# Conditioning loads between the output weight tiles of the first FFN: one load per place, the gate's rows apart from its chunks, intervals of 0.88 tiles

## The chip, the cores and the metric

The kernel runs on one core of a Trainium2 chip. The time is device microseconds of one launch. The kernel before takes 1496.64 us, the median of three runs (1495.39 to 1496.93). One more execution was taken with the hardware profiler; all rows and times below come from it.

## What is computed

Two transformer blocks over 512 tokens of width 1024, in float32. Each block has a mixer (a gated linear recurrence in the first, dilated attention in the second) and a SwiGLU feed-forward layer (FFN). Six vectors per block, made from the conditioning input `c`, scale, shift and gate what goes in and out of the two halves:

```
cond = jax.nn.silu(c)
for layer in range(DEPTH):
    mod = (cond @ ada_w[layer] + ada_b[layer])[:, None, :]
    sh1, sc1, g1, sh2, sc2, g2 = jnp.split(mod, 6, axis=-1)
    u = rms_norm(h, norm_g[layer, 0]) * (1.0 + sc1) + sh1
    ...
    h = h + (1.0 + g1) * rms_norm(y, norm_g[layer, 1])
    u = rms_norm(h, norm_g[layer, 2]) * (1.0 + sc2) + sh2
    y = (jax.nn.silu(gate) * up) @ w_out          # gate, up = split(u @ w_in)
    h = h + (1.0 + g2) * rms_norm(y, norm_g[layer, 3])
```

A vector is a pair (layer, v), with v = 0 to 5 for sh1, sc1, g1, sh2, sc2, g2. The change concerns three of them, which are made while the first FFN (layer 0) multiplies by its output weights `ffn_w_out[0]`: the gate (0, 5), needed at the end of that FFN, and the scale (1, 1) and the shift (1, 0), needed when the attention's input is formed right behind it.

## The kernel before

**Products.** Matmuls run in a split form: a float32 operand x is cut into hi = round(x) (line 90, on ACT) and lo = x - hi (line 91, on DVE), and `three` (lines 586 to 588) adds hi x hi, lo x hi and hi x lo. The second half of the first FFN multiplies the 22 blocks of the hidden activations (`mid`, cut into `oh` by ACT at line 582 and `ol` by DVE at line 583, a ring of five) by 11 tiles of output weights, 1 MB each; the text calls them T0 to T10. A tile is 48 matmuls of 512 columns.

**The stream of weights.** `Stream` walks a fixed list of items. A weight item ("w") is loaded by SP into one of two raw buffers, cut by ACT and DVE into one of three pairs of parts, and then used by PE. Items that load nothing ("do") take no buffer. So with two raw buffers, an item's load is issued when the last reader of the item two loads earlier is done, and SP issues in the order of the list. ACT, DVE and POOL also work in a fixed order, which a scheduler sets when the program is built; from line 978 on, and at the ends of the FFNs, it is written out by hand (`manual_schedule`).

**Conditioning.** A vector's product with `ada_w` is cut into two halves of 512 columns and each half into two chunks of 512 rows, 1 MB each. A chunk takes a raw buffer and four DVE operations: one multiplies its first 128 rows by `cond` (line 401, or 403 if it continues a sum), the others multiply and add (line 403). After a half's second chunk POOL sums over the 128 partitions (line 405). Then comes a finishing step: for the gate, two rows (bias and norm weight, 512 columns each, broadcast to all partitions: two loads at line 64 into one raw buffer) and two DVE operations (lines 450 and 451); for the scale and the shift, four pairs of small DVE operations that turn the row into columns (line 415) and one or two that add the bias and the norm weight (lines 419 and 421).

The text calls the gate's chunks g00, g01 (first half), g10, g11 (second half) and its rows G0, G1; the second half of the scale's chunks s10, s11, with finishing step S1 (its first half is made earlier, between the FFN's input weights); the shift's chunks b00, b01, b10, b11 with finishing steps B0 and B1. V0 and V1 are the first two weight tiles of the attention, which follow in the list.

`weave(ws, others, first, every)` makes the list: after the weight tile with number i it puts the next groups of `others` for as long as i is at least `first` plus `every` times the number of groups already put:

```
for i, w in enumerate(ws):
    res.append(w)
    while i >= first + n * every and o:
        res += o.pop(0)
        n += 1
return res + [i for g in o for i in g]
```

For this place the list was

```
T0 g00 | T1 g01 | T2 g10 | T3 G0 g11 | T4 s10 | T5 G1 s11 | T6 b00 | T7 S1 b01 | T8 b10 | T9 B0 b11 | T10 B1 | V0 V1
```

**The turn.** At the end of the FFN (from `mm(0)` on) the order is written out. PE finishes token block t (`mm(t)`, which uses T9 and T10); ACT squares the result (line 622), DVE multiplies it by the gate (`yg`, line 631), POOL raises the sum to the power -1/2 (`rr`, line 637), DVE adds into the residual (`h`, line 647), ACT squares that, DVE and POOL make the next factor, DVE scales the block (`xn`, line 661), and PE transposes it (`flip(t)`, line 667, eight transposes). ACT and DVE then apply the scale and shift columns (lines 677 and 679), cut the result into `uh` and `ul` (lines 682 and 686), and PE multiplies it by V0 and V1 (`v_prod(t)`). The columns of (1, 0) and (1, 1) have to be complete before line 677 first runs. PE's order there is: mm(0), mm(1), first half of mm(2), flip(0), first half of mm(3), second half of mm(2), flip(1), second half of mm(3), v_prod(0), flip(2), v_prod(1), flip(3), v_prod(2), v_prod(3).

Of the kernel before, what the change touches and what calls it, by code (L numbers as in the profile page):

```python
# [301 lines left out]
def block_kernel(tc, x, c, positions, ada_w, ada_b, norm_g, hgrn_w_in, lower, hgrn_norm_g, hgrn_w_out,  # L302
# [8 lines left out]
    with ExitStack() as ctx:  # L311
# [150 lines left out]
        def ada_seq(*vecs):  # L462

            res, last = [], None
            for l, v in vecs:
                for hf in range(2):
                    res.append([ada_item(l, v, hf, 0)])
                    res.append(([fin_item(*last)] if last else []) + [ada_item(l, v, hf, 1)])
                    last = (l, v, hf)
            return res + [[], [fin_item(*last)]]  # L470

        def ada_halves(l, v):

            return [[ada_item(l, v, hf, kq)] for hf in range(2) for kq in range(2)], [fin_item(l, v, hf) for hf in range(2)]
# [11 lines left out]
        def weave(ws, others, first, every=1):  # L486

            res, o, n = [], list(others), 0
# [7 lines that stand above are left out]
        items = []  # L496
# [11 lines left out]
        def ffn_ws(l):  # L508

            a, w = [], ffn_w_in[l]  # L510
            for j in range(PLAIN[l]):
                a += [win(w, j * 256), win(w, DFF + j * 256)]
            for f in range(2 * PLAIN[l], NF):
                a.append(("quarters", tuple(w[:, c:c + P].rearrange("(k p) n -> p k n", p=P) for c in (DFF + f * P, f * P))))
            return a, [wrow(ffn_w_out[l], j) for j in range(NF // 2)]

        items += weave(hg, ada_seq((0, 2), (0, 4), (0, 3), (1, 4)), 1, 0.7) + hg_o
        f0a, f0b = ffn_ws(0)
        n0 = 2 * PLAIN[0]
        gate, gate_fins = ada_halves(0, 5)  # L520
        one, two = ada_seq((1, 1)), ada_seq((1, 0))
        items += weave(f0a[:n0], [one[0], one[1], [], one[3][:1]], 2) + f0a[n0:]
        late = [gate[0], gate[1], gate[2], gate_fins[:1] + gate[3], one[2], gate_fins[1:] + one[3][1:], two[0], one[5] + two[1]]
        items += weave(f0b, late + two[2:], 0, 0.95)
        AW = attn_w_in[0]

        def av(g, hf):
# [30 lines left out]
        late = ada_seq((1, 2), (1, 3))  # L558
# [780 lines left out]
        early, late = slice(0, 256), slice(256, S)  # L1339
# [1062 lines left out]
        for kind, g, i in order:  # L2402
            if kind == "v":
                steps += [("v", None, None, k, *p) for k, p in enumerate(value_unit(g - 1, i))]
            else:
                two = sevens(g, i) if by_seven(g) else plain(g, i)
# [120 lines left out]
```

## Time and profile before

| | |
|---|---|
| median of three runs | 1496.64 us |
| the profiled execution, its own time | 1492.7 us |
| its span, first to last instruction | 1491.0 us |
| PE busy | 1467.8 us |
| the output weights' part of the first FFN, T0 to mm(3) | 536.9 to 662.2 us of the span |
| PE's waits between 520 and 780 us | 3.8 us: 3.1 for lo of line 91, 0.7 for xn of line 661 |

A row of the timeline has the start, the time in us, the engine, the line of the code and the operation, what it writes and reads, how many are merged, and in brackets how long the engine had been idle before it and what released it. Engines: PE multiplies, ACT is ScalarE, DVE is VectorE, POOL is GpSimd, SPq is the queue from which loads are issued. A matmul of 512 columns is shown with 0.39 us but the next starts 0.227 us after it, since they overlap. T4 to T10 are the rows of line 90 at 576.33, 587.02, 598.99, 609.42, 618.59, 627.85 and 637.11 us, V0 that at 640.74 us.

### The profile page before, as it was taken

Reading aid. Unit: us, or ns where it says so; the run is one execution under the profiler, and the core shown is the slowest. Engines: PE = TensorE matmul, PEld = TensorE weight load, DVE = VectorE, ACT = ScalarE, POOL = GpSimd, SP = SyncE. Lnnn points to the kernel's source line nnn. Section 1 sums busy time; section 2 is a strip of 40 time slices with the busy share of each in tenths; the row PEclk is TensorE's granted clock in tenths of the full one; section 3 lists DMA queues with packets and bytes.
Section 4 is the critical chain, followed back from the end, with each engine's and each line's share of the span. In section 5 each row is a group of like instructions: output and inputs, shape, how many; then the busy total and the mean of one; then the engine's idle time right before and its main releaser. Section 6 shows DMA issues by size and latency. Waiting matters only on the chain. (4 is left out here: it accounts for less than half of the span.)

```text
span 1491.0 us, 25093 instructions
## 1 busy us (share of the span) xinstructions
PE 1467.8 (98%) x9835; PEld 1315.0 (88%) x9835; DVE 1090.9 (73%) x1796; ACT 793.6 (53%) x1470; POOL 191.2 (13%) x172
## 2 busy tenths in 40 slices
PE   8999999999999999999999999999999999999998
PEld 6777788888999988788998999999988899999886
DVE  4587678488688875777798877888776978887533
ACT  4433343373455542257647878567885555555231
POOL 1011112031111100131001010001012211110100
PEclk9999999999999999999999999999999999999999
DMA  9654554115334346644344443354352333334531
GB/s 308 183 175 132 193 170 165 62 59 167 86 114 114 114 149 206 218 141 142 111 118 123 135 121 93 86 163 126 88 199 82 112 88 114 114 114 144 193 116 57
DMA packets 210727, 201.08 MB, mean 135 GB/s; under 512 B 8824, under 2 KB 168496, under 8 KB 210352
## 3 DMA queue, kind: packets, MB, share of 16 engines
q1 hardware_dynamic: 207632, 192.71, 41.5%
q10 hardware_dynamic: 1952, 6.65, 1.2%
q8 instruction: 77, 1.26, 0.3%
q0 software_dynamic: 1024, 0.12, 0.2%
q14 instruction: 42, 0.34, 0.1%
HBM read 192.30 MB, written 5.30 MB: 133 GB/s over the span
## 5 line engine op out<-in xcount | busy, mean ns | idle before, releaser
L90 ACT CAST hi<-raw 128x2048 fp32r<-128x2048 f32 x43 | 82.3, 1913 | 149.3 <-DMA raw<-in_ffn_w_out_dram 78.0
L91 DVE TENSOR_TENSOR lo<-raw,hi 128x2048 fp32r<-128x2048 f32 x43 | 101.8, 2370 | 65.6 <-ACT hi L90 65.6
L586 PE MATMUL ps_mm<-uh,hi 128*128 128x512 f32 (+1 forms) x400 | 145.4, 364 | 0.0
L587 PE MATMUL ps_mm<-ul,hi 128*128 128x512 f32 (+1 forms) x400 | 144.3, 361 | 1.1 <-DVE ul L686 1.1
L588 PE MATMUL ps_mm<-uh,lo 128*128 128x512 f32 (+1 forms) x400 | 143.7, 359 | 0.0
L1988 PE MATMUL ps_mm<-apart,hiq 128*128 128x256 f32 (+1 forms) x608 | 142.3, 327 | 0.3 <-ACT xs L2103 0.2
L1988 PEld LDWEIGHTS ps_mm<-apart,hiq 128*128 128x128 f32 x608 | 99.9, 189 | 8.8 <-ACT xs L2103 0.7
L1988 PE MATMUL ps_mm<-apart,loq 128*128 128x256 f32 (+1 forms) x304 | 97.5, 321 | 0.5 <-DVE loq L2125 0.5
L958 DVE TENSOR_TENSOR loq<-raw,hiq 128x1024 fp32r<-128x1024 f32 x68 | 80.2, 1221 | 22.3 <-ACT hiq L954 22.3
L967 PE MATMUL ps_mm<-th,hiq 128*128 128x256 f32 x340 | 93.8, 276 | 0.0
L967 PE MATMUL ps_mm<-tl,hiq 128*128 128x256 f32 x340 | 93.8, 276 | 0.0
L967 PE MATMUL ps_mm<-th,loq 128*128 128x256 f32 x340 | 93.8, 276 | 0.0
L586 PEld LDWEIGHTS ps_mm<-uh,hi 128*128 128x128 f32 x400 | 75.1, 188 | 18.3 <-issue 6.7
L587 PEld LDWEIGHTS ps_mm<-ul,hi 128*128 128x128 f32 x400 | 75.3, 188 | 12.3 <-DVE ul L686 1.5
L588 PEld LDWEIGHTS ps_mm<-uh,lo 128*128 128x128 f32 x400 | 75.1, 188 | 12.4 <-issue 1.1
L587 PE MATMUL ps_mm<-lo,oh 128*128 128x512 f32 x208 | 81.2, 390 | 3.1 <-DVE lo L91 3.1
L938 POOL TENSOR_TENSOR raw<-raw 128x512 f32<-128x512 f32 x34 | 44.9, 1320 | 301.8 <-DVE loq L934 142.5
L586 PE MATMUL ps_mm<-hi,oh 128*128 128x512 f32 x208 | 81.1, 391 | 0.0
L954 ACT CAST hiq<-raw 128x1024 fp32r<-128x1024 f32 x68 | 68.1, 1047 | 20.8 <-DVE raw L942 19.2
L1988 PE MATMUL ps_mm<-uh,hiq 128*128 128x256 f32 x256 | 71.8, 281 | 0.0
L1988 PE MATMUL ps_mm<-ul,hiq 128*128 128x256 f32 x256 | 71.2, 278 | 0.0
L1988 PE MATMUL ps_mm<-uh,loq 128*128 128x256 f32 x256 | 71.2, 278 | 0.0
(484 smaller groups left out, 4612.9 us busy)
## 6 DMA issues: line engine op xcount, KB each, us to landing
raw<-in_ada_w_dram SPq DMA_DIRECT2D x40, 1024.0 KB, 5.1
raw<-in_ffn_w_in_dram SPq DMA_DIRECT2D x136, 256.0 KB, 4.1
raw<-in_ffn_w_out_dram SPq DMA_DIRECT2D x22, 1024.0 KB, 4.9
raw<-in_attn_w_in_dram SPq DMA_DIRECT2D x64, 256.0 KB, 4.6
raw<-in_hgrn_w_in_dram SPq DMA_DIRECT2D x12, 1024.0 KB, 5.3
raw<-in_attn_w_in_dram SPq DMA_DIRECT2D x12, 1024.0 KB, 5.2
raw<-in_ffn_w_in_dram SPq DMA_DIRECT2D x10, 1024.0 KB, 6.3
raw<-in_attn_w_in_dram SPq DMA_DIRECT2D x16, 512.0 KB, 4.6
```

Source lines behind the costliest of these rows:

```text
L90: self.nc.scalar.copy(hi, t)
L91: self.nc.vector.tensor_sub(lo, t, hi.bitcast(F32))
L586: pe.matmul(ps, ah, bh, start=start, stop=False, skip_group_check=part)
L587: pe.matmul(ps, ah, bl, start=False, stop=False, skip_group_check=part)
L588: pe.matmul(ps, al, bh, start=False, stop=stop, skip_group_check=part)
L938: pool.tensor_add(r[:, 2], r[:, 2], r[:, 0])
L954: act.copy(hi, src)
L958: dve.tensor_sub(lo, src, hi.bitcast(F32))
L967: pe.matmul(ps, w[x][:, a], us[kt][y], start=begin and kt + m == 0, stop=kt == 3 and m == 2, skip_group_check=True)
L1988: pe.matmul(dst(), x, y, start=begin and i == 0, stop=i == len(todo) - 1, skip_group_check=True)
```

## The change

The gate's rows G0 and G1 become groups of their own instead of being put with the chunk behind them, and the spacing goes from 0.95 to 0.88 tiles, since there are now two groups more:

```diff
-        late = [gate[0], gate[1], gate[2], gate_fins[:1] + gate[3], one[2], gate_fins[1:] + one[3][1:], two[0], one[5] + two[1]]
-        items += weave(f0b, late + two[2:], 0, 0.95)
+        late = [gate[0], gate[1], gate[2], gate_fins[:1], gate[3], one[2], gate_fins[1:], one[3][1:], two[0], one[5] + two[1]]
+        items += weave(f0b, late + two[2:], 0, 0.88)
```

The list becomes

```
T0 g00 | T1 g01 | T2 g10 | T3 G0 | T4 g11 | T5 s10 | T6 G1 | T7 s11 | T8 b00 S1 b01 | T9 b10 | T10 B0 b11 B1 | V0 V1
```

No instruction is added or taken away. What moves is the order of the loads on SP, and with it the order of ACT's, DVE's and PE's work on them. Three places follow, before and after; a name such as `raw_5302` is a buffer of one build, and its number differs between the two.

The first place is SP's queue from G0 to T6. Before (G0 in two loads, g11, T4, s10, T5, G1 in two loads, s11, T6):

```order
L64 DMA raw_5202<-in_ada_b_dram 128x512
L64 DMA raw_5202<-in_norm_g_dram 128x512
L70 DMA raw_5209<-in_ada_w_dram 128x4x512
L70 DMA raw_5302<-in_ffn_w_out_dram 128x2x1024
L70 DMA raw_5309<-in_ada_w_dram 128x4x512
L70 DMA raw_5315<-in_ffn_w_out_dram 128x2x1024
L64 DMA raw_5377<-in_ada_b_dram 128x512
L64 DMA raw_5377<-in_norm_g_dram 128x512
L70 DMA raw_5384<-in_ada_w_dram 128x4x512
L70 DMA raw_5444<-in_ffn_w_out_dram 128x2x1024
```

Now (G0 in two loads, T4, g11, T5, s10, T6, G1 in two loads):

```order
L64 DMA raw_5202<-in_ada_b_dram 128x512
L64 DMA raw_5202<-in_norm_g_dram 128x512
L70 DMA raw_5209<-in_ffn_w_out_dram 128x2x1024
L70 DMA raw_5302<-in_ada_w_dram 128x4x512
L70 DMA raw_5308<-in_ffn_w_out_dram 128x2x1024
L70 DMA raw_5371<-in_ada_w_dram 128x4x512
L70 DMA raw_5377<-in_ffn_w_out_dram 128x2x1024
L64 DMA raw_5439<-in_ada_b_dram 128x512
L64 DMA raw_5439<-in_norm_g_dram 128x512
```

T4 stands one load earlier, T5 one, and T6 two (a chunk and G1).

The second place is SP's queue from T8 to V0. Before (T8, b10, T9, b11, T10, V0):

```order
L70 DMA raw_5525<-in_ffn_w_out_dram 128x2x1024
L70 DMA raw_5598<-in_ada_w_dram 128x4x512
L70 DMA raw_5604<-in_ffn_w_out_dram 128x2x1024
L70 DMA raw_5666<-in_ada_w_dram 128x4x512
L70 DMA raw_5672<-in_ffn_w_out_dram 128x2x1024
L70 DMA raw_5744<-in_attn_w_in_dram 128x4x512
```

Now (T8, b00, b01, T9, b10, T10, b11, V0):

```order
L70 DMA raw_5512<-in_ffn_w_out_dram 128x2x1024
L70 DMA raw_5575<-in_ada_w_dram 128x4x512
L70 DMA raw_5581<-in_ada_w_dram 128x4x512
L70 DMA raw_5643<-in_ffn_w_out_dram 128x2x1024
L70 DMA raw_5660<-in_ada_w_dram 128x4x512
L70 DMA raw_5666<-in_ffn_w_out_dram 128x2x1024
L70 DMA raw_5728<-in_ada_w_dram 128x4x512
L70 DMA raw_5734<-in_attn_w_in_dram 128x4x512
```

Two chunks stand between T8 and T9, b11 stands behind T10 instead of ahead of it, and as many loads as before stand ahead of V0.

The third place is DVE's queue where the turn begins. Before, B1 (the four pairs of line 415 and line 419) stands ahead of V0's lo (line 91), and then comes the first gating (line 631):

```order
L415 ISA diag_5808,cols<-shared,ident 128x128
L415 ISA cols 128x1
L415 ISA diag_5810,cols<-shared,ident 128x128
L415 ISA cols 128x1
L415 ISA diag_5812,cols<-shared,ident 128x128
L415 ISA cols 128x1
L415 ISA diag_5814,cols<-shared,ident 128x128
L415 ISA cols 128x1
L419 TENSOR_TENSOR cols<-cols,adab 128x4
L91 TENSOR_TENSOR lo_5818<-raw_5744,hi_5817 128x2048
L631 TENSOR_TENSOR yg_5866<-ps_mm_5095,gate_5299 128x512
```

Now b11's four operations (line 403) and V0's lo come first, and B1 is spread through the turn's first block:

```order
L403 SCALAR_TENSOR_TENSOR shared<-raw_5728,cond,shared 128x512 x4
L91 TENSOR_TENSOR lo_5818<-raw_5734,hi_5817 128x2048
L415 ISA diag_5808,cols<-shared,ident 128x128
L415 ISA cols 128x1
L415 ISA diag_5810,cols<-shared,ident 128x128
L415 ISA cols 128x1
L631 TENSOR_TENSOR yg_5866<-ps_mm_5095,gate_5299 128x512
L415 ISA diag_5812,cols<-shared,ident 128x128
L415 ISA cols 128x1
L635 TENSOR_SCALAR rv_5868<-ss_5861 128x1
L631 TENSOR_TENSOR yg_5872<-ps_a_5099,gate_5299 128x512
L415 ISA diag_5814,cols<-shared,ident 128x128
```

Two pairs of B1 moved behind V0's lo and ahead of the first gating, one pair to between the gating and the factor, and the last, with line 419, behind the second gating.

## The prediction

> **What bounds the kernel now.** I read the page's totals first, then the windows around the change, then PE's timeline where it stands still, and last the queues that feed it.
>
> ```profile
> PE 1467.8 (98%) x9835; PEld 1315.0 (88%) x9835; DVE 1090.9 (73%) x1796; ACT 793.6 (53%) x1470; POOL 191.2 (13%) x172
> ...
> 536.90:640.00 103.10, 101.12 (x447) 83.27 (x445) 71.55 (x109) 31.02 (x33) 16.19 (x5) 1.00 0.61 206
> 640.00:652.00 12.00, 10.89 (x49) 8.79 (x48) 10.22 (x22) 5.83 (x13) 1.44 (x3) 1.00 0.56 178
> 652.00:676.00 24.00, 23.25 (x120) 19.33 (x118) 17.79 (x38) 17.34 (x44) 11.24 (x17) 1.00 0.14 45
> ```
>
> PE is busy 98% of the span, so the kernel is a string of matmuls and an edit that removes none can win back only PE's idle time. In the output weights' stretch (first window: length, then PE's busy time) that is 2 us of 103; in the first 12 us of the turn 1.1 us. Where it lies:
>
> ```profile
> 604.59 0.50 PE L587 MATMUL ps_mm<-lo,oh 128*128 128x512 f32 x1 [1.98 <-DVE lo L91]
> 641.39 0.50 PE L587 MATMUL ps_mm<-lo,oh 128*128 128x512 f32 x1 [1.11 <-DVE lo L91]
> 652.19 0.60 PE L667 MATMUL ps_mm<-ident,xn 128*128 128x128 f32 x4
> 667.60 0.60 PE L667 MATMUL ps_mm<-ident,xn 128*128 128x128 f32 x4
> 674.84 0.66 PE L667 MATMUL ps_mm<-ident,xn 128*128 128x128 f32 x4 [0.75 <-DVE xn L661]
> ```
>
> PE waits 1.98 us for T6's lo and 1.11 us for T10's, 3.1 us together: all that the change can win. The last three rows are flip(0), flip(2) and flip(3). What do the flips have to spare? DVE's rows of the turn:
>
> ```profile
> 641.86 0.29 DVE L415 CUSTOM_DVE_ANT_0 diag<-shared,ident 128x128 f32<-128x128 f32 x1
> ...
> 643.20 0.16 DVE L419 TENSOR_TENSOR cols<-cols,adab 128x4 f32<-128x4 f32 x1
> 643.27 2.29 DVE L91 TENSOR_TENSOR lo<-raw,hi 128x2048 fp32r<-128x2048 f32 x1
> 645.48 0.68 DVE L631 TENSOR_TENSOR yg<-ps_mm,gate 128x512 f32<-128x512 f32 x1
> 646.21 0.68 DVE L631 TENSOR_TENSOR yg<-ps_a,gate 128x512 f32<-128x512 f32 x1
> 647.01 1.42 DVE L647 SCALAR_TENSOR_TENSOR h<-yg,rr,h 128x512 f32<-128x512 f32 x2
> 650.16 0.75 DVE L661 TENSOR_SCALAR xn<-h,rr 128x1024 f32<-128x1024 f32 x1 [0.67 <-POOL rr L637]
> 666.58 0.75 DVE L661 TENSOR_SCALAR xn<-h,rr 128x1024 f32<-128x1024 f32 x1
> ```
>
> xn(0) ends at 650.91 and PE comes to flip(0) at 652.19: 1.3 us to spare. xn(2) ends at 667.33, flip(2) is at 667.60: 0.3 us. For xn(3) PE waits 0.75 us. So by the end of the turn **the bound is the chain of DVE, ACT and POOL through the turn**, not PE, and that chain starts where V0's lo ends (643.27 + 2.29) and the first gating begins. A PE that reaches the turn earlier finds the same chain. What counts is when the chain starts and how long its first steps are.
>
> **The load stream.** SP's issues (g11's, then T5's with G1 behind it, then T7 to V0, b00 among them), and ACT's cuts of T5, T8 and V0:
>
> ```profile
> 567.54 0.38 SPq L70 DMA_DIRECT2D raw<-in_ada_w_dram  x1
> ...
> 580.82 0.37 SPq L70 DMA_DIRECT2D raw<-in_ffn_w_out_dram  x1
> 584.30 0.34 SPq L64 DMA_DIRECT2D raw<-in_ada_b_dram  x1
> ...
> 604.57 0.37 SPq L70 DMA_DIRECT2D raw<-in_ffn_w_out_dram  x1
> 608.40 0.37 SPq L70 DMA_DIRECT2D raw<-in_ada_w_dram  x1
> 613.69 0.37 SPq L70 DMA_DIRECT2D raw<-in_ffn_w_out_dram  x1
> ...
> 622.86 0.37 SPq L70 DMA_DIRECT2D raw<-in_ffn_w_out_dram  x1
> ...
> 632.11 0.37 SPq L70 DMA_DIRECT2D raw<-in_ffn_w_out_dram  x1
> 635.61 0.37 SPq L70 DMA_DIRECT2D raw<-in_attn_w_in_dram  x1
> ...
> 587.02 1.92 ACT L90 CAST hi<-raw 128x2048 fp32r<-128x2048 f32 x1 [5.96 <-DMA raw<-in_ffn_w_out_dram]
> 618.59 1.91 ACT L90 CAST hi<-raw 128x2048 fp32r<-128x2048 f32 x1 [6.22 <-DMA raw<-in_ffn_w_out_dram]
> 640.74 1.91 ACT L90 CAST hi<-raw 128x2048 fp32r<-128x2048 f32 x1 [1.20 <-DMA raw<-in_attn_w_in_dram]
> ```
>
> T8 is issued at 613.69 and its cast starts at 618.59: 4.9 us. Cast 1.9 and lo 2.3 us later its buffer is free, and T9 is issued at 622.86: 9.2 us a tile, as from T9 to T10 (9.25). So the stream runs at the round trip of a tile's buffer, the chunk in the other buffer being hidden in it, as long as one load stands between two tiles.
>
> **Part 1, one load per place.** G1 and a chunk between T3 and T6 go behind them. T4 takes the place that g11 had (567.54); at 9.2 us each T5 follows at 576.7, T6 at 585.9, T7 at 595.1 (before: 604.57), T8 at 604.3. Every lo is then ready before PE asks; T6's and T10's waits go: **PE gains 3.1 us up to the turn**, and comes to flip(0) at 652.19 - 3.1 = 649.1.
>
> **Part 2, two chunks behind T8.** With 0.88, b00 and b01 fall into one place. b01 goes into T8's buffer when its lo is done (604.3 + 9.2 = 613.5). T9 must wait for b00's four operations, which stand behind T8's lo, one cut of `mid` (0.6 us) and mixed with S1:
>
> ```profile
> 605.06 0.28 DVE L415 CUSTOM_DVE_ANT_0 diag<-shared,ident 128x128 f32<-128x128 f32 x1
> ...
> 608.30 0.15 DVE L419 TENSOR_TENSOR cols<-cols,adab 128x4 f32<-128x4 f32 x1
> ```
>
> The same mixture took 3.3 us here, so T9 is issued at about 613.5 + 0.6 + 3.3 = 617.5, T10 at 626.7, and V0, in the same buffer, at 636. Before it was 635.61: **the 9 us that the stream had won at T7 are gone at V0**, since as many loads lie ahead of it. V0 then lands 5.1 us later (as 635.61 to 640.74) at 641.1, its cast ends at 643.0, and its lo starts there or, with eight round trips at up to 9.25 us, 0.4 to 0.6 us later; before it started at 643.27. Term: +0.2 us. The other end: if T9 were issued right behind b01, V0 would come 3.5 us sooner, but B1 stands ahead of the first gating and has to wait for POOL's sum (643.1, part 3); the first gating could then start at 643.9 instead of 645.48, and less the other 0.4 us of B1 the chain would win 1.1 us. I take +0.2, the buffers' own time.
>
> **Part 3, B1 moves into the chain.** Four pairs at 0.33 us (a quarter of 641.86 to 643.20) and line 419: 1.4 us. Before they ran ahead of V0's lo, where DVE would have had to wait for V0's cast till 642.65 in any case. Now two pairs (0.66) stand ahead of the first gating, one (0.33) ahead of the factor, and the last behind the second gating, where DVE waits 0.2 us for POOL anyway (646.21 + 0.60 to 647.01), so 0.1 of it counts. Term: **+1.1 us**. Its sum over partitions must be ready:
>
> ```profile
> 633.26 2.32 DVE L403 SCALAR_TENSOR_TENSOR shared<-raw,cond,shared 128x512 f32<-128x512 f32 x3
> 635.67 3.24 POOL L405 PARTITION_ALL_REDUCE shared<-shared  x1 [14.58 <-DVE shared L403]
> ```
>
> T10's lo ends at 635.9, one cut (0.6) and b11's four operations (0.77 each) follow to about 639.8, POOL takes 3.2 us to 643.1, and the first pair is due at 645.6. If that cover of 2.5 us were gone, each us late would be a us of the chain.
>
> **Part 4, what the new neighbours cost.** G1 is now issued 3 us behind T6. Before it stood 3.5 us behind T5, which took 6.2 us to land (580.82 to 587.02) instead of 4.9. Bounds 0 and 1.3 us, nothing below; I take 0.6. And POOL's sums:
>
> ```profile
> 576.40 3.23 POOL L405 PARTITION_ALL_REDUCE shared<-shared  x1 [19.13 <-DVE shared L403]
> 600.15 3.23 POOL L405 PARTITION_ALL_REDUCE shared<-shared  x1 [20.51 <-DVE shared L403]
> ...
> 578.27 2.52 DVE L91 TENSOR_TENSOR lo<-raw,hi 128x2048 fp32r<-128x2048 f32 x1 [2.05 <-ACT hi L90]
> 600.94 3.59 DVE L91 TENSOR_TENSOR lo<-raw,hi 128x2048 fp32r<-128x2048 f32 x1 [0.89 <-ACT hi L90]
> ```
>
> A lo beside a sum took 2.52 us (1.4 us together) and 3.59 us (2.4 us together) instead of 2.29. In the new order S1's sum (from 608.5) and B0's (from 622) reach 0.6 us each into the lo of T8 and T9. Bounds 0 and 1.3 us; at this overlap nearer the first row: 0.3 us for both. The Trainium skill ("SBUF — State Buffer", "Who interferes with whom") says that a DVE operation with two SBUF inputs and a GpSimd one that reads SBUF share a port pair and that the loser blocks fully. By that the 3.59 would have been 4.7, so the trace does not agree in size; by the rule this term would be 1.2 and the sum 0.9 higher.
>
> **The sum.** 0.2 + 1.1 + 0.6 + 0.3 = 2.2 us later through the chain, which carries flip(2) and flip(3); the 3.1 us that PE wins turn into a wait of 653.1 - 649.1 = 4.0 us at flip(0). Behind flip(3) the queues are in the old order and PE is full, so the 2.2 us stay. The profiled execution would go from 1492.7 to 1494.9; the median stands 3.9 us above that execution, and I add the same 2.2 us: **1498.8 us**.
>
> **The rivals.**
>
> *PE keeps what it wins* (1493.5 us; part of it, 1495.5). For it: both waits do go. Against: flip(2) and flip(3) wait for xn already, and V0 has as many loads ahead. Whole gain 0.05, the early V0 of part 2 (gain up to 1.1) or a zero 0.10.
>
> *The clock falls in the new wait* (slower, decided at flip(0)).
>
> ```profile
> 1484.09 0.39 PE L588 MATMUL ps_b<-hi,ol 128*128 128x512 f32 x1
> ...
> 1486.00:1488.40 2.40, 0.00 (x0) 0.00 (x0) 1.52 (x3) 0.00 (x0) 0.13 (x1) 0.99 0.26 97
> 1488.40:1491.00 2.60, 0.00 (x0) 0.00 (x0) 0.00 (x0) 0.00 (x0) 0.00 (x0) 0.50 0.30 112
> ```
>
> The last matmul ends at 1484.48, and the granted clock is 0.99 until 1488.4 and 0.50 after it: it halved 3.9 us after PE stopped. The new wait is 4.0 us, at the point from which this decides. No row shows a return; if the half rate lasts as long as the fall took, 3.9 us, it costs 1.9 us, of which PE has about 1.0 to spare before flip(2) (653.1 + 15.4 = 668.5 against xn(2) at 669.5). So 2.2 + 0.9 = 3.1, 1499.7 us, and 1501 if it stays twice as long. Chance 0.22. The Trainium skill ("TensorE: Matmul & The Clock Gate", Part 1) has the clock gated to half after an idle window of 3.4 us that runs freely, and released after one busy window; the trace's 3.9 us agree, and by it the cost would be 1.7 us before the spare time.
>
> *The stretch of lo and loads is at its upper bounds* (1.3 for G1, 1.3 for a lo): 0.2 + 1.1 + 2.6 = 3.9, 1500.5 us. For it: each was seen once at that size. Chance 0.15.
>
> *The edit doesn't do what it says*: it holds for T0 to T7, not for T8; that is in the forecast.
>
> **How the numbers follow.** Forecast 0.48, of which 0.08 lies over +3 us. 0.2% (3 us) is about what a measurement of this kernel can tell from no change. Slower by more: 0.08 + 0.19 of the clock + 0.15 = 0.42. Faster by more: 0.05. Within: 0.53. The likeliest case alone spans 1497.4 to 1500.2; with the early V0 below and clock and stretch above the range is 1495.6 to 1501.6.
>
> **What would show it.** No wait for lo of line 91 in T4 to T10; T8's issue near 604 and T9's 13 us behind it; V0's lo starting at 643 to 645; line 415 between the two gatings; a wait of 3.5 to 5 us for xn at flip(0) and about 1 us at flip(2) and flip(3). I am wrong if V0's lo starts before 642, if flip(0) waits under 2 us, or if flip(3) comes earlier than 674.8.

## The result, and the profile after

The changed kernel takes 1500.87 us (median of 7 runs, 1498.13 to 1502.85) and the kernel before 1496.64 us (7 runs beside it, 1495.27 to 1498.14): ratio 1.0032, 95% interval 1.0022 to 1.0041. A second measurement on another chip gave 1.0033 (1.0020 to 1.0045). The change makes the kernel 4 to 5 us slower. The time lies in the forecast range (1495.6 to 1501.6), but 2.1 us above the forecast of 1498.8: not the case called likeliest (within 0.2% of before) came, but the one with 0.42 (slower by more).

The profiled execution took 1500.58 us (span 1498.9). T3's lo, the last tile before the lists differ, ran at 565.22 before and runs at 567.94 now, so this execution was 2.7 us behind before the change had done anything: the granted clock was halved twice for 3.4 us, at 15 and 152 us, which the profiled execution of before does not show. All comparisons below are therefore counted from T3's lo.

PE's waits between 520 and 700 us (the view of waits: who waited for what, us, times, longest):

```profile
engine line waited for: us in total, times, longest us
PE ps_mm L667 <- DVE xn L661: 7.0, 1, 7.0
```

Both waits for lo of line 91 are gone, as forecast, and in their place stands one of 7 us for xn(0), where 4.0 was forecast. PE's rows of flip(0) to flip(3), first four transposes of each:

```profile
657.85 1.11 PE L667 MATMUL ps_mm<-ident,xn 128*128 128x128 f32 x4 [6.97 <-DVE xn L661]
...
667.12 0.60 PE L667 MATMUL ps_mm<-ident,xn 128*128 128x128 f32 x4
...
676.17 0.60 PE L667 MATMUL ps_mm<-ident,xn 128*128 128x128 f32 x4
...
682.52 0.60 PE L667 MATMUL ps_mm<-ident,xn 128*128 128x128 f32 x4
```

From T3's lo, flip(0) came at 86.97 us before and comes at 89.91 now, flip(2) at 102.38 and 108.23, flip(3) at 109.62 and 114.58: 2.9, 5.9 and 5.0 us later. The transposes of flip(0) last 1.11 us instead of 0.60. The windows around them (length, then busy time of PE, PEld, DVE, ACT and POOL, then the granted clock, the DMA share and GB/s) say why:

```profile
640.00:650.88 10.88, 10.88 (x49) 8.66 (x47) 7.10 (x14) 3.07 (x5) 3.23 (x1) 1.00 0.67 202
650.88:653.61 2.73, 0.00 (x0) 0.00 (x0) 0.38 (x3) 0.00 (x0) 0.34 (x1) 1.00 0.94 354
653.61:657.85 4.24, 0.00 (x0) 0.00 (x0) 2.51 (x6) 2.54 (x8) 0.81 (x2) 0.50 0.00 0
657.85:663.85 6.00, 6.00 (x18) 5.06 (x19) 4.83 (x11) 3.79 (x10) 1.42 (x3) 0.50 0.00 0
```

The clock falls to half 2.7 us after PE stopped and stays there for 10.24 us, 6.0 of them with PE at work. That was a rival of the prediction. Of the 3.0 us by which the wait is longer than the 4.0 forecast, 0.9 come from a PE that is earlier than forecast; the other 2.0 are a chain that is 4.2 us late instead of 2.2, and the largest part of that was not in the prediction. POOL's last sum and the first factor (`rr`) of the turn:

```profile
643.13 3.23 POOL L405 PARTITION_ALL_REDUCE shared<-shared  x1 [14.37 <-DVE shared L403]
653.27 0.59 POOL L637 TENSOR_TENSOR rr<-rv,expo 128x1 f32<-128x1 f32 x1 [6.91 <-issue]
```

and DVE's rows of the same place, from V0's lo to xn(0), and xn(2):

```profile
646.68 2.29 DVE L91 TENSOR_TENSOR lo<-raw,hi 128x2048 fp32r<-128x2048 f32 x1 [3.64 <-ACT hi L90]
...
649.44 0.68 DVE L631 TENSOR_TENSOR yg<-ps_mm,gate 128x512 f32<-128x512 f32 x1
...
650.25 0.21 DVE L635 TENSOR_SCALAR rv<-ss 128x1 f32<-128x1 f32 x1
650.37 0.68 DVE L631 TENSOR_TENSOR yg<-ps_a,gate 128x512 f32<-128x512 f32 x1
...
653.90 1.41 DVE L647 SCALAR_TENSOR_TENSOR h<-yg,rr,h 128x512 f32<-128x512 f32 x2 [2.64 <-POOL rr L637]
...
657.04 0.76 DVE L661 TENSOR_SCALAR xn<-h,rr 128x1024 f32<-128x1024 f32 x1 [0.67 <-POOL rr L637]
```

rv is there at 650.46. rr starts at 653.27. POOL's sum ended at 646.36, so POOL did nothing that the profile shows for 6.9 us, with its operand ready for the last 2.8 of them ("issue": nothing recorded was waited for). Before, the sum ended at 635.67 + 3.24, and rr stood at

```profile
646.38 0.60 POOL L637 TENSOR_TENSOR rr<-rv,expo 128x1 f32<-128x1 f32 x1 [7.47 <-DVE rv L635]
```

7.5 us apart too, but there rr comes 0.1 us behind rv (646.29): the pause, if there is one, was just hidden. Up to line 647 the chain is 4.2 us later than before (85.96 against 81.79 from T3's lo), and 2.64 of it is this wait.

### The profile page after: what moved, and what is told of

Same layout as the page of the kernel before. It is cut to its first block, busy times and chain, and to the rows that moved or that the text cites. A ratio compares the mean times of both kernels' runs of the same rounds, so it can differ in the third digit from the quotient of the medians.

```text
span 1498.9 us, 25094 instructions
## 1 busy us (share of the span) xinstructions
PE 1471.7 (98%) x9835; PEld 1318.9 (88%) x9835; DVE 1089.8 (73%) x1796; ACT 793.1 (53%) x1470; POOL 189.9 (13%) x172
```

## The experiments

Three causes were to be told apart: the **chain** (V0's lo later, B1's columns inside, as forecast), POOL's **switch** (a pause of about 7 us behind a sum over partitions, which b11's later sum pushes into the turn), and the **clock** that falls in PE's wait. Ratios are to the kernel before on the same chip (1495.2 to 1495.6 us there).

**1. The changed kernel without POOL's sum of b11** (half of the shift stays unsummed):

```diff
-                if kq == 1 and not sum_by_pe(l, v, hf):
+                if kq == 1 and not sum_by_pe(l, v, hf) and (l, v, hf) != (1, 0, 1):
```

> The changed kernel without POOL's sum over partitions of b11 (the last chunk of the shift; half of that vector stays unsummed, every instruction on DVE is left as it is). If POOL is busy for about 7 us behind such a sum before its next ordinary operation, rr of token tile 0 comes 0.6 to 1 us behind rv instead of 2.8 us, xn(0) and flip(0) 2.7 us earlier, PE's wait at flip(0) is 4.2 us instead of 7.0, and the half clock lasts at most 3.4 us or does not come: 1497.0 to 1498.5 us. If only V0's lo and the four column pairs make the chain late, nothing changes: wait of 7 us, 1500.9 us.

Ratio 1.0006 (0.9995 to 1.0016). POOL's rr comes 0.1 us behind rv, and PE waits less:

```profile
652.15 0.66 PE L667 MATMUL ps_mm<-ident,xn 128*128 128x128 f32 x4 [2.59 <-DVE xn L661]
```

flip(3) is at 109.62 us from T3's lo, where it was before the change. But this takes three things away: with no sum to wait for, the scheduler put B1's columns ahead of V0's lo, so they left the chain as well, and V0's lo started at 78.08 us from T3's lo, as before the change (78.05), where the changed kernel has 78.74. That is why the wait is 2.6 and not 4.2. The half clock lasted 3.4 us. Sum, columns and V0's lo together carry nearly all of the loss; runs 3, 4 and 5 part them.

**2. PE kept busy in the wait**, measured twice, the second time beside the changed kernel on the same chip:

```diff
-                    n.flip(0, [bank("mm"), bank("a")])
+                    b0 = [bank("mm"), bank("a")]
+                    for k in range(26):
+                        pe.matmul(b0[1], parts[NF - 4][0][:, 0:P], ws[0][0][:, 0:512], start=True, stop=True)
+                    n.flip(0, b0)
```

> The changed kernel with 26 more matmuls of 0.23 us (5.9 us together) on PE just ahead of flip(0), into the bank that flip(0) overwrites. If the clock that falls in PE's wait costs part of the time, the granted clock stays at 1.0 through flip(0) to flip(3), flip(0) comes at the same time, flip(2) 2 to 3 us earlier, and the time is 1498 to 1499 us. If only the late chain costs, flip(2) and flip(3) stay where they are and the time stays 1500.9 us. If the matmuls themselves delay flip(0), it is over 1501 us.

> The changed kernel itself, once more, on the chip of the next two: ratio 1.0025 to 1.004 to the kernel before, POOL's rr 6.9 to 8 us behind the sum's end, half clock in the wait at flip(0).

> The 26 extra matmuls ahead of flip(0) again, beside the changed kernel on one chip, for the price of the half clock. From the medians so far it is 2 us (ratio 0.0014 lower than the change), from the two single traces 0.5 us at flip(3) (the chain of xn(3) follows 0.5 us behind PE in any case). If the ratio is within 0.0007 of the change's, the half clock costs no more than 1 us and the late chain is all; if it is 0.001 to 0.002 lower, the clock costs 1.5 to 3 us.

Ratios 1.0018 (1.0009 to 1.0027) and 1.0014 (1.0005 to 1.0023), beside 1.0033 (1.0020 to 1.0045) for the change itself: matmuls that compute nothing make the kernel 2.5 us faster (1498.20 against 1500.69). The windows of the second of these runs, with the clock at 1.00 throughout, and its flips:

```profile
650.50:657.00 6.50, 5.98 (x27) 4.58 (x26) 2.52 (x6) 2.54 (x8) 1.14 (x2) 1.00 0.32 125
657.00:664.00 7.00, 7.00 (x38) 5.99 (x39) 4.82 (x11) 4.81 (x12) 2.41 (x4) 1.00 0.00 0
```

```profile
656.99 0.66 PE L667 MATMUL ps_mm<-ident,xn 128*128 128x128 f32 x4 [0.52 <-DVE xn L661]
...
673.40 0.66 PE L667 MATMUL ps_mm<-ident,xn 128*128 128x128 f32 x4 [0.79 <-DVE xn L661]
...
680.85 0.65 PE L667 MATMUL ps_mm<-ident,xn 128*128 128x128 f32 x4 [0.89 <-DVE xn L661]
```

flip(2) is 106.4 us from T3's lo instead of 108.2 or 108.6, and flip(3) 113.9 instead of 114.6 or 115.0. With the full clock PE waits for xn(2) and xn(3) again, so the chain takes back half of what the clock gives: at flip(3) the half clock costs only 0.5 to 1.1 us, taking each of the two traces with it against each of the two without. The rest of the 2.5 us appears 140 us later. Between 780 and 830 us PE is idle for 2.4 and 3.9 us in the two traces of the changed kernel, 0.9 and 1.2 in the two with the extra matmuls, 1.8 before; the longest waits there are for ACT in the attention. That idle time does not follow the half clock in the turn: it is 1.0 us in run 5's first version, with 6.8 us of half clock, and 2.3 in run 7, with none there. So only the part at flip(3) is shown to be the price of the half clock; what ties the later place to the turn was not tried.

**3. The kernel before with a second sum over partitions** behind b11's (a maximum over rows that are equal by then):

```diff
+                if kq == 1 and (l, v, hf) == (1, 0, 1):
+                    pool.partition_all_reduce(a, a, P, bass.bass_isa.ReduceOp.max)
```

> The kernel before with a second sum over partitions of b11 right behind the first (as a maximum over rows that are equal by then, so that no value changes). It ends 3.2 us after the first, at about 642.2 on the clock of the profile of before, still 3.5 us ahead of rv at 645.9. If POOL needs 6.9 us behind such an operation, rr comes at 649.1 instead of 646.4, xn(0) 2.7 us later, PE waits about 1.4 us at flip(0), and flip(2) and flip(3) are 2 to 2.7 us later: 1498.5 to 1499.3 us. If POOL is free when the operation ends, rr is where it was and the time is that of before.

Ratio 1.0025 (1.0014 to 1.0036). POOL's rows (line numbers are two higher in this kernel):

```profile
637.66 3.23 POOL L405 PARTITION_ALL_REDUCE shared<-shared  x1 [14.55 <-DVE shared L403]
640.99 3.88 POOL L407 PARTITION_ALL_REDUCE shared<-shared  x1
652.86 0.59 POOL L639 TENSOR_TENSOR rr<-rv,expo 128x1 f32<-128x1 f32 x1 [8.00 <-issue]
```

The second sum follows the first at once; only the return to an ordinary operation takes 8.0 us. rr is 4.3 us later than before (85.47 against 81.16 from T3's lo). Of this 0.9 is another effect: B1's columns now wait for the second sum, so V0's lo and with it rv are 0.9 us later (rv 81.73 against 80.87). The other 3.4 are POOL's pause, with rv long there. PE waits 3.2 us at flip(0), the clock halves for 3.4 us, and flip(3) is 4.3 us later. The mechanism is as expected, the size larger: the pause is not a constant, and it brings the half clock with it. Nothing of the load order was changed here: a sum on POOL that ends later makes the kernel before nearly as slow as the change does, and most of that is the pause.

**4. V0's cut behind xn(0)**, in the changed kernel, and alone in the kernel before. `take` stops one tile earlier, and the cut is written into the turn:

```diff
-                ws = [st.take(), st.take(1)]
+                ws = [st.take(2 if l else 1), st.take(1 if l else 0)]
+                if l == 0:
+                    st.process_to(st.wpos[st.taken])
...
                     n.xn(0)
+                    st.process_to(st.wpos[st.taken] + 1)
```

> The changed kernel with V0's cut moved behind xn(0), and POOL's sum of b11 left where it is. rv of token tile 0 then comes 1.7 us earlier. If V0's lo and the column pairs set the late chain, rr, xn(0) and flip(0) come 1.7 us earlier and the ratio falls from 1.0032 to about 1.002. If POOL's 6.9 to 8 us behind the sum set it, rr comes 6.9 to 8 us behind the sum's end as before, flip(0) does not move by more than 0.5 us, and the clock halves again; ratio 1.003, or more, since V0's lo now stands behind xn(0).

> The kernel before with V0's cut moved behind xn(0) and nothing else. PE's waits for the lo of T6 and T10 stay; the chain starts up to 1.3 us earlier (mm(0) ends at about 644.1, the first gating stood at 645.48), but POOL is not ready before about 645.8 to 646.9 if it needs 6.9 to 8 us behind the sum that ends at 638.9. Wait of 0.75 us at flip(3) gone, ratio 0.999 to 1.000. It says how much of f1's time comes from the late cut alone.

In the changed kernel: ratio 1.0039 (1.0024 to 1.0054). DVE's first factor, and POOL's sum and rr:

```profile
645.34 0.21 DVE L635 TENSOR_SCALAR rv<-ss 128x1 f32<-128x1 f32 x1
```

```profile
640.18 3.23 POOL L405 PARTITION_ALL_REDUCE shared<-shared  x1 [14.64 <-DVE shared L403]
651.14 0.59 POOL L637 TENSOR_TENSOR rr<-rv,expo 128x1 f32<-128x1 f32 x1 [7.72 <-issue]
```

rv is 2.2 us earlier than in the changed kernel (80.07 against 82.31 from T3's lo) and rr is not (85.87 against 85.33). A chain that starts sooner wins nothing while POOL holds rr: this parts switch and chain. Two other readings of the pause fall here as well. The sum was really over at the end of its row, since DVE's first column operation, which reads it, starts 0.04 us later (643.45 against 643.41). And DVE did not hold POOL up, since DVE itself stood idle for 5.6 us of the pause, waiting for rr. In the kernel before: ratio 1.0012 (1.0003 to 1.0021), slightly slower, where 0.999 to 1.000 was expected. There too rr starts 7.0 us behind the sum's end, and 0.8 us after its rv was there, so **the kernel before already stood at the edge of the switch**. V0's lo behind xn(0) then makes PE wait 1.81 us at flip(2), and the wait at flip(3) stays (0.79).

**5. b11 summed on PE** with four small matmuls against the column `expo` (-0.5) and one DVE operation, no POOL sum and no column pairs:

```diff
+                    b0 = [bank("mm"), bank("a")]
+                    a = accs.pop((1, 0, 1))
+                    for k in range(4):
+                        pe.matmul(b0[1][:, k:k + 1], a[:, k * P:(k + 1) * P], expo[:, 0:1], start=True, stop=True)
+                    dve.scalar_tensor_tensor(cols[:, 4, 4:8], b0[1][:, 0:4], -2.0, abc(1, 0)[:, 4:8], op0=OP.mult, op1=OP.add)
```

First it was put right ahead of flip(0):

> The changed kernel with b11's sum over partitions made by four small matmuls on PE ahead of flip(0) and one DVE operation in place of the four pairs of line 415: POOL's last sum is then B0's, 17 us earlier, and no column of the shift stands in the chain. What is left of the change is V0's lo 0.7 us later. If switch, columns and clock are all there is, xn(0) comes 3.7 us earlier than in the changed kernel, PE waits about 3 us at flip(0) with no half clock, and the time is that of before or up to 1 us above: 1496.5 to 1497.7 us. If the load stream or the gate's rows cost something that was not seen, it stays over 1498 us.

Ratio 1.0010 (0.9999 to 1.0020). This place has a cost of its own: the DVE operation then stands behind token block 1's two updates in DVE's queue, so flip(0)'s second half waited 1.75 us for it, with 6.8 us of half clock. Then behind mm(1):

> The changed kernel with b11 summed on PE behind mm(1) as in the version that beat both, and V0's cut left ahead of the first gating. POOL's switch and the columns are gone and only V0's late lo is left of the change: xn(0) as late as in the kernel before plus 0.7 us, PE waits 2.5 to 3.5 us at flip(0), flip(3) up to 0.7 us later than before, ratio 1.000 to 1.0008. If it falls to 0.998 the late cut was not needed for the gain; if it stays over 1.002 switch and columns were not what made the change slower.

Ratio 0.9992 (0.9983 to 1.0001). From T3's lo rr is at 81.87 (before 81.16) and flip(3) at 110.37 (109.62): 0.7 us later, just V0's late lo, as expected. PE's wait came elsewhere: 1.61 us ahead of the sum's matmuls, which follow the gating, and under 0.5 us at flip(0), where 2.5 to 3.5 were expected. The ratio is nevertheless a little lower than expected; its interval reaches to 1.0001, and PE's idle time at 780 to 830 us is 0.8 us here against 1.8 before.

**6. Both together**, the sum on PE behind mm(1) and V0's cut behind xn(0), in the changed kernel:

> The changed kernel with b11 summed by four small matmuls and one DVE operation, placed behind mm(1) in program order (no sum on POOL behind B0's), and with V0's cut (hi and lo) moved behind xn(0). Then nothing stands ahead of the first gating but PE's own mm(0), which in the changed kernel's trace ended 8 us ahead of flip(0)'s place in PE's row. If the chain's start was all that was late, PE keeps the 3.1 us that it won and does not wait at flip(0), flip(2) or flip(3): 4 to 5 us under the kernel before, ratio 0.9967 to 0.998. If the work moved behind xn(0) makes xn(2) and xn(3) late instead, PE waits at flip(2) or flip(3) and the ratio is 0.999 to 1.001.

Ratio **0.9972** (0.9962 to 0.9982), 1491.68 us against 1495.6: it beats both kernels. Its flips (line 669 here):

```profile
650.68 0.60 PE L669 MATMUL ps_mm<-ident,xn 128*128 128x128 f32 x4
...
666.70 0.66 PE L669 MATMUL ps_mm<-ident,xn 128*128 128x128 f32 x4 [0.45 <-DVE xn L663]
...
674.05 0.66 PE L669 MATMUL ps_mm<-ident,xn 128*128 128x128 f32 x4 [0.78 <-DVE xn L663]
```

The first gating starts at 75.65 us from T3's lo (81.50 in the changed kernel, 80.26 before), PE goes into flip(0) without a wait and the clock stays at 1.00. flip(3) is at 107.63, 2.0 us earlier than in the profiled execution of before. Of the 3.9 us between the medians that leaves 1.9; 0.8 of it is the idle time at 780 to 830 us (1.0 against 1.8), the rest is not placed. The old list with both edits was not run, so that PE's gain comes from the new list is read from the trace (no wait for a lo, flip(0) at 84.26 us against 86.97) and not from a run.

**7. One chunk ahead of T0**, so that no place has two chunks and b11 stands ahead of T10 again:

```diff
-        late = [gate[0], gate[1], gate[2], gate_fins[:1], gate[3], one[2], gate_fins[1:], one[3][1:], two[0], one[5] + two[1]]
-        items += weave(f0b, late + two[2:], 0, 0.88)
+        items += gate[0]
+        late = [gate[1], gate[2], gate_fins[:1] + gate[3], one[2], gate_fins[1:], one[3][1:], two[0], one[5] + two[1]]
+        items += weave(f0b, late + two[2:], 0, 0.95)
```

> The change with its first chunk (g00) moved ahead of T0 and the rows G0 again beside g11, spacing 0.95: one load per place from T3 on, no place with two chunks behind T8, and b11 again ahead of T10. T9 then follows T8 by 9.2 us, V0 is issued some 4 us earlier than in the changed kernel, b11's sum ends 9 us earlier, POOL is free before rv, and the columns run ahead of V0's lo. If the load ahead of T0 costs PE nothing, PE keeps what it won: ratio 0.997 to 0.999. If T0's or T3's lo comes late for it, PE waits there and the ratio is 1.000 or above.

Ratio 1.0031 (1.0022 to 1.0041): the second of the two outcomes. PE's waits between 525 and 560 us:

```profile
PE ps_mm L587 <- ACT hi L90: 2.8, 1, 2.8
PE ps_mm L968 <- ACT ps_mm L1010: 0.7, 1, 0.7
PE ps_mm L588 <- DVE lo L91: 0.7, 1, 0.7
```

With g00 ahead of T0, T1 is issued at 548.60 us instead of 531.74, and PE stands still 3.5 us for its parts (lines 587 and 588, one higher in this kernel; the other wait is of the loop before). The granted clock is then at half from 556.7 to 563.5 us, 6.8 us. So this version loses its time 100 us ahead of the turn. The whole stream is late with T1, and b11's sum ends at 647.3 us, not 9 us earlier as expected; rr comes 0.1 us behind rv and 6.9 us behind the sum. Nothing follows from this run for the switch.

What the traces have in common, in us from T3's lo of each execution (run 7 is left out, since there T3 itself is moved):

| kernel | ratio | rr(0) | wait at flip(0) | half clock | flip(3) |
|---|---|---|---|---|---|
| before | 1 | 81.16 | 0 | 0 | 109.62 |
| the change (two traces) | 1.0032, 1.0033 | 85.33, 85.76 | 6.97, 6.96 | 10.2 | 114.58, 114.95 |
| change, PE kept busy (two) | 1.0018, 1.0014 | 85.62, 85.44 | 1.00, 0.52 | 0 | 114.06, 113.88 |
| change, V0 cut late | 1.0039 | 85.87 | 6.99 | 6.8 | 116.98 |
| before, two sums | 1.0025 | 85.47 | 3.21 | 3.4 | 113.90 |
| change, no POOL sum of b11 | 1.0006 | 81.19 | 2.59 | 3.4 | 109.62 |
| change, sum on PE ahead of flip(0) | 1.0010 | 81.66 | 2.39 and 1.75 | 6.8 | 112.36 |
| change, sum on PE behind mm(1) | 0.9992 | 81.87 | under 0.5 (1.61 at the sum) | 0 | 110.37 |
| before, V0 cut late | 1.0012 | 81.00 | 0 | 0 | 112.11 |
| change, sum on PE, V0 cut late | 0.9972 | 76.55 | 0 | 0 | 107.63 |

rr is at 85.3 to 85.9 wherever a sum on POOL ends behind 75 us, whatever stands ahead of it on DVE, and at 81 to 82 or below where it does not.

## Why the prediction was right or wrong

**What bounds the kernel: right.** PE's gain did turn into a wait at flip(0), and what sets the turn is when the chain of DVE, ACT and POOL gets through. The version that let the chain start early is the only one that kept PE's gain.

**Part 1, right in kind.** The waits for T6's and T10's lo are gone. Counted from T3's lo, PE was through with its products ahead of flip(0) 4.0 us earlier (at 650.88 against 652.19, and this execution is 2.72 us behind), 0.9 more than the 3.1 of the two waits.

**Part 2, right, with V0 later than forecast.** SP's issues of T8, of b00 and b01 (two merged), of T9 and of V0:

```profile
608.07 0.37 SPq L70 DMA_DIRECT2D raw<-in_ffn_w_out_dram  x1
612.17 5.41 SPq L70 DMA_DIRECT2D raw<-in_ada_w_dram  x2
621.04 0.37 SPq L70 DMA_DIRECT2D raw<-in_ffn_w_out_dram  x1
...
639.42 0.37 SPq L70 DMA_DIRECT2D raw<-in_attn_w_in_dram  x1
```

T9 follows T8 by 12.97 us (forecast 13), and V0 goes out at 636.7 on the clock of before (636). V0's lo is 0.7 us later than before, where this part had 0.2; what it lacked comes from part 4.

**Part 3, the columns right, the cover wrong.** B1's columns stand where the order had them, and put rv 0.75 us further behind the start of V0's lo (3.57 against 2.82 us); with the last pair behind the second gating 0.84 where 1.1 was forecast. But the part asked only whether the sum's result would be ready for the columns, and gave it "that cover of 2.5 us". The reader of POOL's queue that mattered was rr, which stands behind the sum on the same engine. The prediction took POOL to be free when the sum's row ends. The row of before that could have warned, rr [7.47 <-DVE rv] behind the sum, looks like POOL waiting for DVE. **This is the missing term: 2.64 us.** The Trainium skill ("GPSIMD Engine Reference", "2.1 Instruction dispatch") says that the first call to a freshly loaded kernel on this engine pays a code load of about 6 us that no instruction in the profile shows; if rr behind a sum counts as such a call, it would by this have been due about 6 us after the sum's end (an estimate from that page). The traces agree in kind, with 6.8 to 8.0 us in the seven traces where the pause can be seen, but no run shows that code is loaded in it. The prediction did not weigh it.

**Part 4, G1's cost came by another way, the sums cost nothing.** G1 did not slow T6's load (issued at 588.59, its cast at 593.50: 4.9 us). But the first of the gate's finishing operations (line 450) stands ahead of T6's lo in DVE's order, and it waited for G1's bias row:

```profile
593.50 1.91 ACT L90 CAST hi<-raw 128x2048 fp32r<-128x2048 f32 x1 [4.75 <-DMA raw<-in_ffn_w_out_dram]
...
595.82 0.69 DVE L450 TENSOR_TENSOR gate<-shared,raw 128x512 f32<-128x512 f32 x1 [3.30 <-DMA raw<-in_ada_b_dram]
596.43 2.29 DVE L91 TENSOR_TENSOR lo<-raw,hi 128x2048 fp32r<-128x2048 f32 x1
```

The cast ended at 595.41, so T6's lo was 1.0 us late, and T8 went out at 605.35 on the clock of before instead of 604.3. At V0 0.7 us of it were left. The prediction had 0.6 for G1, from a slower load. Every lo from T4 to V0 took 2.29 us, so the sums beside them cost 0 where 0.3 was forecast.

**The sum.** 0.69 for V0's lo, 0.84 for the columns and 2.64 for POOL make the 4.17 us later at line 647, of which flip(0) shows 2.9, since PE had 1.3 us to spare there. The forecast of 2.2 was somewhat high in the terms that it had: 0.7 for the whole stream up to V0's lo, where it had 0.2 + 0.6 + 0.3, and 0.84 for the columns instead of 1.1. Together they are 1.5 where it had 2.2, and the missing 2.64 stands beside them.

**The clock, a rival with 0.22, came true**, and for a longer wait than it was worked out for. It put the return at 3.9 or twice that after the fall; it was 10.24 us. And it put its cost at 0.9 us behind the spare time: 0.5 to 1.1 us at flip(3), so the price there was about right, though for a half clock that lasted longer. The medians with and without it differ by 2.5 us, and the rest of that is not explained. The waits of "about 1 us at flip(2) and flip(3)" did not show in the changed kernel, because PE, at half clock, came later than xn(2) and xn(3); with PE kept busy they are there (0.8 and 0.9 us).

That the time lies in the range is in part luck: the range had its upper room for the clock and for a slow stretch of lo and loads, and the pause on POOL, which was in neither, happened to fit into it. The wait at flip(0), 7.0 us where 3.5 to 5 was named as the sign of being right, shows that the chain was not as forecast.

## What to carry to other kernels

Before moving an operation past another on an engine, ask not only when its result is needed but what the engine must do next, and how long it takes to get there: the row to read is the gap between the two on that engine, in the place where it was hidden before. A wait that a change opens on PE should be priced with the clock that may fall in it, and here a wait of 2.6 us was enough. And where a long chain behind a stage has its own start, freeing PE ahead of it is worth nothing until that start is freed too: a late sum taken off POOL and a cut moved out of the chain made a loss of 0.3% into a gain of 0.3%.

## What the runs showed of the hardware that was not expected

- **POOL pauses behind a sum over partitions** before its next ordinary operation, though the sum's result can be read at once: 6.9 and 7.2 us in the change, 7.5 and 6.8 with PE kept busy, 8.0 behind two sums, 7.7 and 7.0 with V0's cut late. Two sums in a row have no pause between them (640.99 behind 637.66 + 3.23). What sets its length from 6.8 to 8.0 us stays open.
- **The half clock comes in pieces of 3.4 us**: 3.4 us after waits of 2.59 and 3.21 us, 6.8 after two waits close together (2.39 and 1.75 us in run 5, 2.77 and 0.67 in run 7), 6.8 or 10.2 after waits of 7 us, none after single waits of up to 2.0 us in the same stretch. The length of the wait alone does not decide: in the attention 3.4 us of half clock came behind waits of 2.15 and 1.94 us (from 822.7 us in run 4's changed kernel and from 822.9 in run 7), and none behind one of 2.24 us in the second trace of the change. After the wait of 2.59 us it began 1.1 us behind PE's restart (653.2, with flip(0) at 652.15). In the changed kernel it ended 6.0 us after PE's restart. The Trainium skill ("TensorE: Matmul & The Clock Gate", Part 1) has a free-running window of 3.4 us, half rate after at least one idle window and full rate after at least one busy one. The pieces and the long return agree with that; that 2.6 us of waiting are enough does not agree with a whole idle window.
